# Gate and up projections of a decoder step: when the normed tokens are asked for, where the last splits stand, and in which order the quarter products run

## The chip, the cores and the metric

One core of a Trainium2 chip. The metric is the device time of one execution in microseconds (us). Engines: TensorE (PE) multiplies and writes accumulators in PSUM, VectorE (DVE), ScalarE (ACT) and GpSimd (POOL) work element by element, SyncE (SP) asks for transfers.

## The reference, cut to what matters

One layer of a decoder for 520 tokens (512 of a prompt, 8 samples), width 1024: mLSTM and retention heads, a cross-attention, and then the part that the change touches, a SwiGLU network of inner width 2816:

```python
hf = rmsnorm(x, g_ffn)
x = x + (jax.nn.silu(hf @ w_gate) * (hf @ w_up)) @ w_down
y = rmsnorm(x, g_final)
```

## The kernel before, in words

All tokens lie feature-major: 128 features on the partitions, 520 tokens along the free dimension, so x is 8 blocks of 128 x 520 (`X`). Each float32 operand of a product is split in a high part (ScalarE copies it to fp32r) and a low part (VectorE subtracts the high part from the raw one), and a product is hi·hi + hi·lo + lo·hi. `split` writes both; its lines are L191 (high) and L192 (low). The weights come in one long stream of blocks (`W`); `W.get` loads a block ahead into `wraw`, casts it (`whi`, L208) and subtracts (`wlo`, L209). A product that is not of the feed-forward's normed tokens but of `A` = x·g (also split) takes the row factors of the norm (`r_bc`, `r_h`) afterwards.

The inner width is 22 blocks of 128 columns. The first four (`PLAIN`) are plain projections: `proj(A, "pfg")` and `proj(A, "pfu")`, 48 matmuls each (8 row blocks, 3 products, 2 halves of 260 tokens), read out of PSUM by L1194 (gate, times the row factors), L1200 (up) and L1201 (their product, after Silu). An accumulator pair comes from `ps2`, of which there are two; the next projection but one needs the one that these lines empty.

Meanwhile the operands of the other 18 blocks are made: `operands` multiplies x by gain and row factors (L1152, eight operations into `xn`), forms sums of quarters (L1157, L1158, L1161, L1164) and splits seven of them into `xs` (`xsplit`). It is a generator: `spawn` puts it on the list of tasks, and each `step` runs it up to its next yield; `proj` makes a step after every second row block but the last.

Blocks 4 to 21 treat gate and up weights as a 2 x 2 matrix of quarters and make its product with the tokens by seven quarter products (j = 0 to 6) of 12 matmuls, with sums before (`weight_operands`: L1175 to L1178, seven splits, for the block after the running one) and after (L1221 to L1234). Products 2 and 3 go to the pair `ab`, 5 and 6 to `cd`, the others to single accumulators.

The results are split again (`ff_split`) as operands of the down projection. Those of the first 8 blocks go to `A` while later blocks run. Those of blocks 8 to 21 go to `TT`, the memory in which `xs` lies, and so can't be written before the last quarter block: `ff_split(KB + z)` writes over the operand of product z // 2. In the last block two of them are written after each product. The down projection follows (L1257; the last row block L1295), reading `A` for its first 8 row blocks and `TT` for the other 14.

The tile framework places the waits and sets the order of each engine's queue when the kernel is built (`schedule_with_timeline_sim=True`), from the order in which the operations are written and from when they are ready; each engine then runs its queue in that order.

Of the kernel before, what the change touches and what calls it, by code (L numbers as in the profile page):

```python
# [13 lines left out]
AF = mybir.ActivationFunctionType  # L14
ALU = mybir.AluOpType
# [10 lines left out]
KB = 8  # L26
# [3 lines left out]
H2 = N // 2  # L30
# [5 lines left out]
FB = DFF // P  # L36
# [79 lines left out]
def halves(ap):  # L116
    return ap.rearrange("p (a b) -> p a b", a=2)
# [23 lines left out]
def decoder_step(ctx: ExitStack, tc: tile.TileContext, i: dict, o: list):  # L141
    nc = tc.nc
    pe, act, dve, pool, sp = nc.tensor, nc.scalar, nc.vector, nc.gpsimd, nc.sync
# [18 lines left out]
    def ps2(name):  # L162
        return acc.tile([P, 2, 512], F32, tag="acc", name=name)

    def ps1(name):
        return psums[-1].tile([P, 512], F32, tag="msc", name=name)
# [21 lines left out]
    def split(hi, lo, src, scale=None):  # L188

        if scale is None:  # L190
            act.copy(hi, src)  # L191
            dve.tensor_tensor(lo, src, hi.bitcast(F32), ALU.subtract)  # L192
        else:
            act.activation(hi, src, AF.Copy, scale=scale)
            dve.scalar_tensor_tensor(lo, src, scale, hi.bitcast(F32), ALU.mult, ALU.subtract)

    def wraw(at, n):
        raw = wp.tile([P, KB * P], F32, tag="wraw", name="wraw", bufs=3)
        sp.dma_start(raw[:, :n], i["weights"][at : at + P * n].rearrange("(p n) -> p n", p=P))
        return raw  # L200
# [29 lines left out]
    def spawn(gen, group=None):  # L230
        tasks.append([gen, 0, group])
# [15 lines left out]
    def proj(x, name, order=range(KB), ahead=1):  # L247
        hi, lo = W.get(ahead)
        ps = ps2(name)
        for n, k in enumerate(order):  # L250
            mm_k(ps, hi, lo, x, k, k, n == 0, n == KB - 1)
            if n % 2 and n < KB - 1:
                step()
        return ps
# [109 lines left out]
    with ExitStack() as mx:  # L364
# [179 lines left out]
        def qkv_tiles(n):  # L544
            return [qkv.tile([P, N], F32, tag=t, name=f"{t}{n}") for t in ("q", "k", "v")]
# [222 lines left out]
        for h in range(4):  # L768
            q, k, v = qkv_tiles(f"m{h}")
# [16 lines left out]
        for h in range(4):  # L786
            q, k, v = qkv_tiles(f"r{h}")
# [7 lines left out]
        for hb in range(KB):  # L795
            ps = proj(A, "pgt")
# [60 lines left out]
    for ob in range(KB):  # L857

        ps = proj(B, "pwo", range(KB) if ob < KB - 1 else (*range(4, KB), *range(4)))
# [244 lines left out]
    for (k0, nk, nc_), need in zip(PASSES, (1, 2, 3)):  # L1104
        while min(done[0], attended[0]) < need or any(t[2] == "mem" for t in tasks):
            step()
        for c0 in range(0, D, nc_):
            hi, lo = W.get()
            for c in range(0, nc_, P):
                ob = (c0 + c) // P  # L1110
                ps = ps2("pwc")
# [23 lines left out]
    FR = fp.tile([P, FB - KB, N], F32, name="FR")  # L1135
# [7 lines left out]
    def ff(s, k, ts):  # L1143
        return A[:, s, k, ts] if k < KB else TT[:, k - KB, s, ts]

    def xsplit(j, x):
        split(*xs[j], x)

    def operands():

        for k in range(KB):
            dve.scalar_tensor_tensor(xn[:, :, k], halves(X[:, k]), vec[:, k, V_GF : V_GF + 1], r_h, ALU.mult, ALU.mult)  # L1152
            if k % 2:
                yield 1
        b11, b21, b12, b22 = (xn[:, a, k : k + 4].rearrange("p k n -> p (k n)") for a in range(2) for k in (0, 4))
        t3 = fr[:, 12 * N : 14 * N]
        dve.tensor_tensor(t3, b22, b12, ALU.subtract)  # L1157
        dve.tensor_tensor(b12, b12, b11, ALU.subtract)  # L1158
        xsplit(0, b11)
        yield 1  # L1160
        dve.tensor_tensor(b11, b22, b12, ALU.subtract)  # L1161
        xsplit(4, b21)
        yield 1
        dve.tensor_tensor(b21, b21, b11, ALU.subtract)  # L1164
        for j, x in ((1, t3), (6, b22), (3, b12), (2, b11), (5, b21)):
            xsplit(j, x)
            yield 1

    def weight_operands(out):

        g, u = (wraw(W.next()[1], KB * P) for _ in range(2))
        yield 1
        s13, s24 = (wp.tile([P, KB * P], F32R, tag=t, name="wsum", bufs=2).bitcast(F32) for t in ("whi", "wlo"))
        a11, a12, a21, a22, s3, s1, s2, s4 = (t[:, z : z + 4 * P] for t in (g, u, s13, s24) for z in (0, 4 * P))
        dve.tensor_tensor(s3, a11, a21, ALU.subtract)  # L1175
        dve.tensor_tensor(s1, a21, a22, ALU.add)
        dve.tensor_tensor(s2, s1, a11, ALU.subtract)
        dve.tensor_tensor(s4, a12, s2, ALU.subtract)  # L1178
        for w in (a11, s3, s2, s1, a12, a22, s4):
            hi, lo = (tp.tile([P, 4 * P], F32R, tag="q" + t, name="q" + t, bufs=8) for t in ("hi", "lo"))  # L1180
            split(hi, lo, w)
            out.append((hi, lo))
            yield 1

    def ff_split(f, raw):
        split(ff(0, f, slice(None)), ff(1, f, slice(None)), raw)

    spawn(operands())
    ops = []
    for f in range(PLAIN):  # L1190
        ps = proj(A, "pfg")
        gu = tp.tile([P, 4, H2], F32, tag="gu", name="gu").rearrange("p (a z) n -> p a (z n)", a=2)
        g, u = gu[:, 0], gu[:, 1]
        dve.tensor_tensor(halves(g), ps[:, :, :H2], r_h, ALU.mult)  # L1194
        act.activation(g, g, AF.Silu)
        if f == PLAIN - 1:
            spawn(weight_operands(ops))
        step()
        ps = proj(A, "pfu", ahead=int(f < PLAIN - 1))
        dve.tensor_tensor(halves(u), ps[:, :, :H2], r_h, ALU.mult)  # L1200
        dve.tensor_tensor(FR[:, f], u, g, ALU.mult)  # L1201
        step()
    drain()
    for f in range(PLAIN, FB):
        last, nxt = f == FB - 1, []
        more = weight_operands(nxt) if not last else iter(())
        next(more, None)
        ab, cd = ps2("pfa"), ps2("pfb")
        ps = [*(ps1(z)[:, :H2] for z in ("pfc", "pfd")), ab[:, 0, :H2], ab[:, 1, :H2], ps1("pfe")[:, :H2], cd[:, 0, :H2], cd[:, 1, :H2]]
        gu = tp.tile([P, 4, H2], F32, tag="gu", name="gu")  # L1210
        g1, g2, v1, v2 = (gu[:, z] for z in range(4))
        for j, (out, (wh, wl), (xh, xl)) in enumerate(zip(ps, ops, xs)):
            for k in range(4):
                for w, x in ((wh, xh), (wh, xl), (wl, xh)):
                    pe.matmul(  # L1215
                        out, w[:, k * P : (k + 1) * P], x[:, k * H2 : (k + 1) * H2],
                        start=k == 0 and w is wh and x is xh, stop=k == 3 and w is wl,
                    )
            next(more, None)
            if j == 0:  # L1220
                act.copy(g1, out)  # L1221
            elif j == 2:
                dve.tensor_tensor(g2, out, g1, ALU.add)
                dve.tensor_tensor(v1, ps[1], g2, ALU.add)
            elif j == 3:
                dve.tensor_tensor(gu[:, 1::2], out.unsqueeze(1).broadcast_to([P, 2, H2]), gu[:, 1:3], ALU.add)  # L1226
            elif j == 4:
                dve.tensor_tensor(g1, out, g1, ALU.add)
                act.activation(g1, g1, AF.Silu)
            elif j == 6:  # L1230
                dve.tensor_tensor(gu[:, 1:3], cd[:, ::-1, :H2], gu[:, 1:3], ALU.add)
                act.activation(g2, g2, AF.Silu)
                to = FR[:, f - KB if f >= KB else f]
                dve.tensor_tensor(halves(to), gu[:, 0:2], gu[:, 2:4], ALU.mult)  # L1234
            if f - PLAIN < KB and j == 5:
                ff_split(f - PLAIN, FR[:, f - PLAIN])
            if last:
                if j == 1:
                    W.fill(1)
                for z in (2 * j, 2 * j + 1):  # L1240
                    ff_split(KB + z, FR[:, z])
        list(more)
        ops = nxt
    tp_cm.__exit__(None, None, None)
# [4 lines left out]
    for obs in ((0, 1), *((ob,) for ob in range(2, KB - 1))):  # L1249
        pss = [ps2("pfd") for _ in obs]  # L1250
        for k0 in range(0, FB, KB):
            for ps in pss:
                hi, lo = W.get()
                for k in range(k0, min(k0 + KB, FB)):
                    for w, s in ((hi, 0), (hi, 1), (lo, 0)):
                        for a in range(2):
                            pe.matmul(  # L1257
                                ps[:, a, :H2], w[:, k - k0], ff(s, k, slice(a * H2, (a + 1) * H2)),
                                start=k == 0 and w is hi and s == 0, stop=k == FB - 1 and w is lo,
                            )  # L1260
        for ob, ps in zip(obs, pss):
            xb = X[:, ob]
            dve.tensor_tensor(halves(xb), halves(xb), ps[:, :, :H2], ALU.add)
            square(yp, ob)
            act.activation(xb, xb, AF.Copy, scale=vec[:, ob, V_GO : V_GO + 1])
# [20 lines left out]
    for n0, n in ((0, H2), (H2, N - H2)):  # L1286
        ts = slice(n0, n0 + n)
        ps = ps2("pfd")[:, 0, :n]
# [84 lines left out]
```

## Time and profile before

| | us |
|---|---|
| median of 3 runs | 884.39 (880.81 to 885.61) |
| the profiled execution | 878.44 |
| its span | 876.7 |
| PE, DVE, ACT busy in it | 835.8, 673.4, 397.5 |

The span goes from the first to the last instruction of the profiled execution; 1.7 us lie around it. A busy engine is one that has an instruction in it: the matmuls are pipelined, so a busy PE is not PE at its peak.

### The profile page before, as it was taken

What the parts mean: (1) busy time and instruction counts of PE and PEld (TensorE: products, weight loads), DVE (VectorE), ACT (ScalarE), POOL (GpSimd) and SP (SyncE); (2) the same over time, 40 slices, a digit from 0 to 9 for tenths busy, and PEclk for the clock granted to TensorE, in tenths of its full rate; (3) what the DMA queues carried; (4) which work ended last, traced back from release to release, by engine and by line L of the source; (5) the groups of instructions that cost most, each with busy time, mean ns of one, the idle gap of its engine ahead of it and who ended that gap; (6) DMA issues with size and microseconds to landing.
All of it is one profiled execution on the core that took longest, in us unless ns stands there. A gap on an engine that the chain in (4) does not pass through costs nothing.

```text
span 876.7 us, 16989 instructions
## 1 busy us (share of the span) xinstructions
PE 835.8 (95%) x6707; PEld 818.4 (93%) x6707; DVE 673.4 (77%) x1512; ACT 397.5 (45%) x791; POOL 179.6 (20%) x185
## 2 busy tenths in 40 slices
PE   6989989999999999999999879999999996999996
PEld 5989989999999999889999879999999996999995
DVE  6999998877786687876888897999999997232234
ACT  5545525434546353365442654555444555132231
POOL 5555332222024301415323400000000000011010
PEclk9999999999999999999999999999999998999998
DMA  8333323434345436784764222223333332222222
GB/s 272 99 97 124 104 76 122 124 99 124 103 146 193 121 124 215 250 301 118 233 208 140 73 66 79 97 97 100 119 119 99 96 105 84 84 91 91 84 67 98
DMA packets 32680, 110.56 MB, mean 126 GB/s; under 512 B 4000, under 2 KB 6176, under 8 KB 32344
## 3 DMA queue, kind: packets, MB, share of 16 engines
q1 hardware_dynamic: 27216, 95.80, 34.5%
q0 software_dynamic: 3616, 12.34, 3.9%
q10 hardware_dynamic: 1768, 1.34, 0.5%
q8 instruction: 53, 0.87, 0.4%
q14 instruction: 27, 0.22, 0.1%
HBM read 100.38 MB, written 9.07 MB: 125 GB/s over the span
## 4 chain that ended last, share of the span: by engine, by line
PE 76%; DVE 15%; DMA 4%; issue 2%; ACT 1%; POOL 1%; SPq 0%; DVEq 0%; ACTq 0%; POOLq 0%
PE pfd L1257 13%; PE pfa L1215 6%; PE pfb L1215 6%; PE pgt L223 5%; PE pcq L223 5%; PE pwo L223 5%; PE pwc L223 4%; PE pfc L1215 3%; PE pfe L1215 3%; PE prp L223 3%; PE ppl L223 3%; PE pfg L223 3%; PE pfd L1215 3%; PE pfu L223 2%; DVE cv L518 2%
## 5 line engine op out<-in xcount | busy, mean ns | idle before, releaser
L208 ACT CAST whi<-wraw 128x1024 fp32r<-128x1024 f32 (+1 forms) x104 | 107.2, 1032 | 179.6 <-PE pfd L1257 69.4
L209 DVE TENSOR_TENSOR wlo<-wraw,whi 128x1024 fp32r<-128x1024 f32 (+1 forms) x85 | 110.3, 1300 | 72.0 <-ACT whi L208 70.2
L302 POOL TENSOR_TENSOR ssq<-ssq,sq 128x520 f32<-128x520 f32 x18 | 28.8, 1600 | 369.1 <-ACT sq L301 363.9
L191 ACT CAST qhi<-wsum 128x512 fp32r<-128x512 f32 x72 | 42.9, 619 | 54.4 <-DVE wsum L1175 45.8
L1257 PE MATMUL pfd<-TT,whi 128*128 128x260 f32 x392 | 62.8, 282 | 0.0
L209 POOL TENSOR_TENSOR wlo<-wraw,whi 128x1024 fp32r<-128x1024 f32 x19 | 45.6, 2398 | 66.2 <-ACT whi L208 61.1
L1215 PE MATMUL pfa<-TT,qhi 128*128 128x260 f32 x288 | 53.7, 284 | 0.0
L1257 PEld LDWEIGHTS pfd<-TT,whi 128*128 128x128 f32 x392 | 53.7, 188 | 0.0
L1215 PE MATMUL pfb<-TT,qhi 128*128 128x260 f32 x288 | 53.0, 283 | 0.0
L192 DVE TENSOR_TENSOR qlo<-wsum,qhi 128x512 fp32r<-128x512 f32 x72 | 47.8, 684 | 0.0
L223 PE MATMUL pwc<-B,whi 128*128 128x260 f32 x256 | 43.7, 287 | 4.0 <-DVE X L291 3.0
L223 PE MATMUL ppl<-A,whi 128*128 128x260 f32 x256 | 45.4, 290 | 0.6 <-DVE up L510 0.6
L223 PE MATMUL pcv<-A,whi 128*128 128x260 f32 x256 | 45.0, 291 | 0.5 <-ACT whi L208 0.5
L1215 PEld LDWEIGHTS pfb<-TT,qhi 128*128 128x128 f32 x288 | 44.5, 188 | 0.0
L1215 PEld LDWEIGHTS pfa<-TT,qhi 128*128 128x128 f32 x288 | 44.4, 188 | 0.0
L223 PE MATMUL prp<-A,whi 128*128 128x260 f32 x256 | 44.2, 288 | 0.0
L223 PE MATMUL pgt<-A,whi 128*128 128x260 f32 x256 | 44.0, 287 | 0.0
L1257 PE MATMUL pfd<-A,whi 128*128 128x260 f32 x224 | 37.1, 289 | 6.0 <-DVE gu L1226 6.0
L223 PE MATMUL pcq<-A,whi 128*128 128x260 f32 x256 | 42.0, 283 | 0.0
L1215 PE MATMUL pfa<-TT,qlo 128*128 128x260 f32 x144 | 41.0, 285 | 0.7 <-DVE qlo L192 0.7
L223 PE MATMUL pwo<-B,whi 128*128 128x260 f32 x256 | 41.3, 283 | 0.0
L1215 PE MATMUL pfb<-TT,qlo 128*128 128x260 f32 x144 | 40.8, 283 | 0.0
(434 smaller groups left out, 2614.2 us busy)
## 6 DMA issues: line engine op xcount, KB each, us to landing
wraw<-in_weights_dram SPq DMA_DIRECT2D x132, 512.0 KB, 3.8
kv<-in_cache_k_dram SPq DMA_DIRECT2D x16, 512.0 KB, 4.5
kv<-in_cache_v_dram SPq DMA_DIRECT2D x16, 512.0 KB, 4.3
wraw<-in_weights_dram SPq DMA_DIRECT2D x8, 384.0 KB, 3.0
X<-in_x_dram SPq DMA_DIRECT2D x2, 1040.0 KB, 6.0
Cs<-in_state_C_dram POOLq DMA_DIRECT2D x4, 512.0 KB, 5.0
out_dram<-Cs POOLq DMA_DIRECT2D x4, 512.0 KB, 3.1
Ss<-in_state_S_dram POOLq DMA_DIRECT2D x4, 512.0 KB, 4.2
```

The costliest lines, as they stand in the source:

```text
L191: act.copy(hi, src)
L192: dve.tensor_tensor(lo, src, hi.bitcast(F32), ALU.subtract)
L208: act.copy(hi[:, :n], raw[:, :n])
L209: (pool if index in LO_ON_POOL else dve).tensor_tensor(lo[:, :n], raw[:, :n], hi[:, :n].bitcast(F32), ALU.subtract)
L223: pe.matmul(ps[:m, a, :H2], w[:, k, c0 : c0 + m], x[:, s, xk, a * H2 : (a + 1) * H2], start=first and w is hi and s == 0, stop=last and w ...
L302: (dve if ob == KB - 1 else pool).tensor_tensor(ssq, ssq, s, ALU.add)
L518: dve.scalar_tensor_tensor(cv[:, :LO], up[:, j : j + LO], wc(j), cv[:, :LO], ALU.mult, ALU.add)
L1215: pe.matmul(out, w[:, k * P : (k + 1) * P], x[:, k * H2 : (k + 1) * H2], start=k == 0 and w is wh and x is xh, stop=k == 3 and w is wl,)
L1257: pe.matmul(ps[:, a, :H2], w[:, k - k0], ff(s, k, slice(a * H2, (a + 1) * H2)), start=k == 0 and w is hi and s == 0, stop=k == FB - 1 and ...
```

## The change

Three things. The generator `operands` is spawned after the first gate block has been read (after L1194 and its Silu), not ahead of the plain blocks; its splits come in the order of the products. The order of the seven quarter products becomes a11, a12, s3, s2, s1, a22, s4 (it was a11, s3, s2, s1, a12, a22, s4), with the readings placed to match. In the last quarter block no results are split before product 4; after products 4, 5 and 6 two each are split (six of the 14), and the other eight within the down projection, one after every second row block; `W.fill(1)` moves from product 1 to product 3.

```diff
         xsplit(0, b11)
         yield 1
         dve.tensor_tensor(b11, b22, b12, ALU.subtract)
-        xsplit(4, b21)
+        xsplit(1, b21)
         yield 1
         dve.tensor_tensor(b21, b21, b11, ALU.subtract)
-        for j, x in ((1, t3), (6, b22), (3, b12), (2, b11), (5, b21)):
+        for j, x in ((2, t3), (3, b11), (4, b12), (5, b21), (6, b22)):
...
-        for w in (a11, s3, s2, s1, a12, a22, s4):
+        for w in (a11, a12, s3, s2, s1, a22, s4):
...
-    spawn(operands())
+    unsplit = list(range(KB, FB))
+
+    def rest_split(n):
+        for _ in range(min(n, len(unsplit))):
+            f = unsplit.pop(0)
+            ff_split(f, FR[:, f - KB])
+
     ops = []
     for f in range(PLAIN):
...
         act.activation(g, g, AF.Silu)
+        if f == 0:
+            spawn(operands())
         if f == PLAIN - 1:
             spawn(weight_operands(ops))
...
-        ps = [*(ps1(z)[:, :H2] for z in ("pfc", "pfd")), ab[:, 0, :H2], ab[:, 1, :H2], ps1("pfe")[:, :H2], cd[:, 0, :H2], cd[:, 1, :H2]]
+        pc, pd, pe_ = (ps1(z)[:, :H2] for z in ("pfc", "pfd", "pfe"))
+        ps = [pc, pd, ab[:, 0, :H2], ab[:, 1, :H2], pe_, cd[:, 0, :H2], cd[:, 1, :H2]]
...
             if j == 0:
-                act.copy(g1, out)
-            elif j == 2:
-                dve.tensor_tensor(g2, out, g1, ALU.add)
-                dve.tensor_tensor(v1, ps[1], g2, ALU.add)
+                act.copy(g2, out)
+            elif j == 1:
+                dve.tensor_tensor(g1, out, g2, ALU.add)
+                act.activation(g1, g1, AF.Silu)
             elif j == 3:
+                dve.tensor_tensor(g2, out, g2, ALU.add)
+                dve.tensor_tensor(v1, ps[2], g2, ALU.add)
+            elif j == 4:
                 dve.tensor_tensor(gu[:, 1::2], out.unsqueeze(1).broadcast_to([P, 2, H2]), gu[:, 1:3], ALU.add)
-            elif j == 4:
-                dve.tensor_tensor(g1, out, g1, ALU.add)
-                act.activation(g1, g1, AF.Silu)
...
             if last:
-                if j == 1:
+                if j == 3:
                     W.fill(1)
-                for z in (2 * j, 2 * j + 1):
-                    ff_split(KB + z, FR[:, z])
+                if j > 3:
+                    rest_split(2)
...
                                 start=k == 0 and w is hi and s == 0, stop=k == FB - 1 and w is lo,
                             )
+                    if k % 2:
+                        rest_split(1)
```

## Rows read from the trace of the kernel before

**Rows 1.** Chain of waits in order of time, 500 to 740: start, us, engine, operation.

```profile
511.16 7.54 PE pfg L223 x48
518.69 5.77 PE pfu L223 x48
...
547.53 1.45 PE pfc L1215 x12
...
630.28 1.44 PE pfd L1215 x12
...
711.08 1.45 PE pfd L1215 x12
...
737.78 2.29 PE pfd L1257 x9
```

**Rows 2.** Whom TensorE waited for: us in total, times, longest.

```profile
PE pfd L1257 <- DVE gu L1226: 6.0, 1, 6.0
PE pfg L223 <- DVE gu L1194: 4.4, 1, 4.4
PE pwc L223 <- DVE X L291: 3.0, 2, 2.7
...
PE pfa L1215 <- DVE qlo L192: 0.7, 1, 0.7
...
PE pfe L1215 <- ACT qhi L191: 0.6, 1, 0.6
```

**Rows 3.** TensorE by stretch: length, busy (count), granted clock, DMA share, GB/s.

```profile
495.00:506.00 11.00, 11.00 (x91) 1.00 0.29 77
...
512.00:515.00 3.00, 3.00 (x16) 0.50 0.00 0
...
738.00:740.00 2.00, 2.00 (x10) 0.50 0.00 0
```

**Rows 4.** VectorE in order of time at the first plain block: start, length.

```profile
506.29 4.11 DVE L1152 SCALAR_TENSOR_TENSOR FR<-X,vec,r_bc 128x520 f32<-128x520 f32 x6
510.32 0.69 DVE L1194 TENSOR_TENSOR gu<-pfg,r_bc 128x520 f32<-128x520 f32 x1
510.93 1.42 DVE L1152 SCALAR_TENSOR_TENSOR FR<-X,vec,r_bc 128x520 f32<-128x520 f32 x2
512.27 0.69 DVE L1200 TENSOR_TENSOR gu<-pfu,r_bc 128x520 f32<-128x520 f32 x1
512.88 1.22 DVE L209 TENSOR_TENSOR wlo<-wraw,whi 128x1024 fp32r<-128x1024 f32 x1
514.01 1.24 DVE L192 TENSOR_TENSOR TT<-FR,TT 128x1040 fp32r<-128x1040 f32 x1
515.16 1.24 DVE L1157 TENSOR_TENSOR FR<-FR 128x1040 f32<-128x1040 f32 x1
```

**Rows 5.** VectorE by stretch, plain blocks: length, busy (count), granted clock, DMA share.

```profile
506.00:534.00 28.00, 27.78 (x32) 0.94 0.21 65
```

**Rows 6.** All engines by stretch, quarter blocks and after: length; PE, PEld, DVE, ACT, POOL.

```profile
559.00:719.00 160.00, 160.00 (x1329) 159.85 (x1329) 152.60 (x270) 78.64 (x158) 0.00 (x0) 1.00 0.33 106
719.00:738.00 19.00, 11.72 (x92) 11.06 (x91) 18.97 (x32) 12.88 (x24) 0.00 (x0) 0.89 0.33 104
738.00:850.00 112.00, 112.00 (x925) 112.00 (x926) 30.59 (x31) 31.38 (x37) 8.70 (x5) 0.99 0.26 82
```

**Rows 7.** VectorE in order of time, last quarter block: first and last splits, readings.

```profile
722.64 1.30 DVE L192 TENSOR_TENSOR TT<-FR,TT 128x520 fp32r<-128x520 f32 x2
...
729.31 0.42 DVE L1223 TENSOR_TENSOR gu<-pfa,gu 128x260 f32<-128x260 f32 x1
...
734.44 0.42 DVE L1224 TENSOR_TENSOR gu<-pfd,gu 128x260 f32<-128x260 f32 x1
...
735.12 1.91 DVE L192 TENSOR_TENSOR TT<-FR,TT 128x520 fp32r<-128x520 f32 x3
736.94 0.69 DVE L1226 TENSOR_TENSOR gu<-pfa,gu 128x520 f32<-128x520 f32 x1
```

## The prediction

> **What bounds the kernel now.** I read the chain of waits in order of time first [rows 1]. From the plain blocks to the end of the down projection it is TensorE nearly throughout: a plain projection of 48 matmuls is 5.77 us, and in the quarter blocks the same product comes round every 10.10 us (630.28 to 711.08 is 8 blocks), with nothing between. So inside this stage a faster VectorE or ScalarE buys nothing; only the places where TensorE stands are worth anything. The second view lists whom TensorE waits for [rows 2]. Its two long waits of this stage are the two that the diff touches: 4.4 us for the reading L1194 of the first gate block and 6.0 us for the reading L1226 of the last quarter block; 0.7 and 0.6 us more stand just ahead of the latter. The third view is the granted clock of stretches [rows 3]: behind both waits TensorE runs at 0.50, the lower level (1.2 GHz), for some three us. Undisturbed it has 1.00 (2.4 GHz), and the 2.7 us wait ahead of the gate projections [rows 2] cost no such thing: the projections from 495 to 506 run at 1.00 [rows 3]. The last views are VectorE's operations in order of time around both waits, and its busy time by stretch [rows 4 to 7].
>
> **The front: normed tokens asked for later.** TensorE finished the first up block at 506.76 (511.16 less the 4.4 us wait), and needs the accumulator that L1194 empties. L1194 had its row factors at 506.29, but six operations L1152 stand ahead of it on VectorE, 4.11 us, so it runs at 510.32 [rows 4]. The change spawns the eight L1152 after L1194. Then L1194 takes 506.29 to 506.98, and 0.15 us later (as 511.01 to 511.16 now) the second gate block starts: 507.13 in place of 511.16, 4.0 us. The wait left is 0.4 us, well under the 2.7 us that left the clock up, so the 48 matmuls take 5.77 us and not 7.54 [rows 1]: another 1.8 us. That block ends at 512.90 and not 518.69, 5.8 us sooner.
>
> Nothing is removed from VectorE, though. It is busy 27.78 of the 28.00 us from 506 to 534 [rows 5], and TensorE now asks sooner. What is late next is the second up block, whose accumulator L1200 frees. Behind L1194 (0.61 us to the next start) stand eight L1152 at 0.685 each (4.11 over 6), so L1200 starts at 512.38, ends at 513.07, and the block starts at 513.2: a wait of 0.3 us. Its weights' low half is next: the high half is cast in time, since the subtraction runs at 512.88 now, right after L1200 [rows 4]; behind L1200 it runs from 512.99 to 514.2, while the block asks for it after four matmuls, at 513.7. That is 0.6 us more. If the first split of the tokens (L192, 1.15 us) gets in ahead of it, 1.75. Then VectorE still has ten or so operations of 1.15 us each, so the reading and the low half for the third gate block may come 0 to 1.6 us late in their turn. I take 0.3, 0.6 and 0.9, together 1.8: they lie between no wait (lower bound 0) and, as upper bound, a wait at each of the five blocks that follow of one 1.15 us operation, 5.8, which would eat everything. By 534 the list is as empty as now, since it holds the same work without a hole in both cases; the quarter blocks' sums (L1175) wait for the fourth gate block and move with TensorE. Front: 5.8 - 1.8 = 4.0 us, bounds 0 and 5.8.
>
> Which order VectorE's queue has decides this. In [rows 4] the low half at 512.88 belongs to the next projection, and yet it stands ahead of L1157, which was written one projection earlier: the scheduler that fills the queues takes what is ready, so a chain of dependent operations (L1157, L1158, L1161, L1164) lets later work in between. That is why I take waits of tenths and not of several operations.
>
> The Trainium skill (TensorE: Matmul & The Clock Gate, section Architectural detail) says that VectorE and ScalarE run their queues as strict FIFO. The trace agrees: L1194, which had all it needed at 506.29, ran behind the six that were queued first. By that rule with a queue filled as written the time would be the first rival's 878.8, with the order that the rows show it is the 873.8 of the sum.
>
> **The middle: plain gate quarters first.** The order of the seven products and of their seven weight operands changes, not their number: 84 matmuls, three 260-wide adds, three 520-wide operations, one copy and two Silu per block as before. The first two products then need only the raw quarters, not sums. Of the accumulators, the pair ab was emptied by operations after products 3 and 4, and now by two adds after product 4; the next block wants it at its product 3, some 7 us later. The pair cd is emptied at product 7 as now. TensorE already fills its 160.00 us of 160 there, VectorE 152.60 [rows 6], so a gain is excluded and a loss needs VectorE to lose its 7.4 us of room. I take 0; bounds 0 and +22 (third rival).
>
> **The end: last splits behind the readings.** Eighteen blocks of 10.10 us from 547.53 end at 729.3; the down projection starts at 737.78 [rows 1], so 8.5 us lie in the last block: 6.0 waiting for L1226, 1.3 for weight operands [rows 2], the rest in small change. VectorE is busy 18.97 us of the 19.00 [rows 6]. Ahead of L1226 it runs 13 of the 14 splits of the down projection's operand, from 722.64 to 735.12, at 0.61 us (1.30 for two, overlapped): 7.9 us. It also shows how a reading gets stuck: L1224 needs only L1223, yet comes 5.1 us behind it (729.31 to 734.44), with splits and others in between [rows 7]. The change writes no split before the operation that frees ab, six after products 5 to 7, and eight into the down projection, where VectorE is busy 30.59 us of 112 [rows 6]. With none ahead, ab would be free at 737.63 - 7.9 = 729.7 and TensorE would go straight on: 8 us. But the splits are ready early (the operand slots are free after each product), and [rows 4] showed that ready work written later still gets in. With 8 ahead the gain is 5 x 0.61 = 3.0. I take four or five ahead: 5.4 us. The remaining wait is then some 3 us or comes in pieces, so the clock stays up: the first 9 matmuls of the restart took 2.29 us [rows 1] at the 0.50 of [rows 3], where 9 x 0.120 (5.77 / 48) are 1.1, so 1.2 us come back. The first split needed in the down projection is of its ninth row block, after 16 row blocks of 0.72 us (5.77 / 8), 11.5 us on; the splits left are 8 x 0.61 = 4.9 us, hidden under that. The first down weights are asked for two products later; they have a whole projection's room. End: 5.4 + 1.2 = 6.6 us, bounds 3.0 and 9.7.
>
> **Sum.** 4.0 + 0 + 6.6 = 10.6 us. The profiled execution took 878.44 (span 876.7) and would take 867.8. The median of the three runs is 884.39, 6 us above it, and the runs spread by 4.8; I put the difference on the median: 873.8 us.
>
> **Rivals.**
> First, the front goes to VectorE: if its queue keeps the written order, the second up block's low half stands behind L1201, L1157, L1158 and a split (0.61 + 3 x 1.15), ends at 518.3 and TensorE waits 4.7 us there, enough to drop the clock as the 4.4 us did. Then the front gives 5.8 - 0.3 - 4.7 - 1.8 = -1.0, the end 6.6: 884.39 - 5.6, about 878.8. For it: the 27.78 of 28.00. Against: the mixed order of [rows 4].
> Second, the end is not what it says: the splits still fill VectorE ahead of the last readings, since they are ready, and nothing holds them back but place in the text. The end then gives about 0.5 of small change, the front 4.0: 879.9. For it: the 18.97 of 19.00 and L1224's delay; against: fewer are written in time.
> Third, on the other side: the new product order makes TensorE wait in each quarter block. The price is that of the last block now, 0.7 + 0.6 [rows 2], where VectorE has no room left: 1.3 us in 17 blocks is 22 us, and less the 10.6 of both ends that is 895.8. It decides from 0.88 us per block on ((10.6 + 4.4) / 17). Against it: VectorE's work per block is the same, with 0.46 us of room (7.4 / 16), and the sums get more time.
> Fourth, both ends come to nothing together: 884.
>
> **How the numbers follow.** A measurement here tells about 0.5% (4.4 us) from no change. Forecast as above: 0.62, range 869 to 879. First rival 0.12 and second 0.14, each a little more often beyond 4.4 us than not; third 0.07; fourth 0.05. Faster: 0.62 + 0.08 + 0.09 = 0.79; same: 0.04 + 0.05 + 0.05 = 0.14; slower 0.07. The range takes in the first two rivals and the largest gains: 867 to 883.
>
> **What would show it.** Right: L1194's successor runs before any L1152, TensorE's wait there falls under 1 us, no stretch at 0.50 follows; waits of some tenths appear for L1200 and low halves of weights in the plain blocks, and the quarter blocks start about 4 us sooner; they still come every 10.10 us; the wait of the first down matmul falls under 3 us, with splits inside the down projection. Wrong: a 4 us wait at the second up block (first rival); 13 splits still ahead of the last reading (second); a period above 10.5 us (third). A shift in stages ahead of 500 us, which the diff does not touch, would be outside all of these.

## The result, and the profile after

The changed kernel takes 877.99 us (median of 11 runs, 874.8 to 882.17), the kernel before 883.97 (11 runs beside it, 880.81 to 887.71): ratio 0.9947, 95% interval 0.9926 to 0.9968, so 0.5% faster, 4.7 us. The two medians lie 6.0 us apart, a little more than the ratio says and inside its interval; from here on the ratio on record is used, and microseconds beside a ratio are that share of some 882 us. Forecast were 873.8 us, 1.2%; the measured median lies inside the range of 867 to 883. The profiled execution took 874.8 us.

```profile
span 873.0 us, 17065 instructions
PE 833.0 (95%) x6707; PEld 816.0 (93%) x6707; DVE 671.6 (77%) x1512; ACT 406.7 (47%) x798; POOL 179.4 (21%) x185
```

That is the head of the page after. ScalarE is busy 9.2 us longer than the 397.5 of before, though no line of the diff gives it work: the first sign of what went wrong.

Lines have moved: L1194 of before is L1200 now, L1200 is L1208, the pair `ab` is read by L1235 and L1236 (it was last read by L1226), `cd` by L1240, the down projection is L1266. The waits of TensorE in the changed stages, after (us in total, times, longest):

```profile
PE pfb L1224 <- DVE gu L1240: 2.4, 1, 2.4
...
PE pfd L1266 <- DVE gu L1236: 1.1, 1, 1.1
...
PE pfg L223 <- DVE gu L1200: 0.4, 1, 0.4
...
PE pfu L223 <- DVE wlo L209: 0.3, 1, 0.3
```

Set beside [rows 2]: the 4.4 us at the first gate block have become 0.4, and the 6.0 us ahead of the down projection 2.4 and 1.1. VectorE at the first plain block, after (start, length), to be held against [rows 4]:

```profile
505.42 0.70 DVE L1200 TENSOR_TENSOR gu<-pfg,r_bc 128x520 f32<-128x520 f32 x1
506.04 5.45 DVE L1152 SCALAR_TENSOR_TENSOR FR<-X,vec,r_bc 128x520 f32<-128x520 f32 x8
511.40 0.69 DVE L1208 TENSOR_TENSOR gu<-pfu,r_bc 128x520 f32<-128x520 f32 x1
512.01 1.21 DVE L209 TENSOR_TENSOR wlo<-wraw,whi 128x1024 fp32r<-128x1024 f32 x1
```

The reading (L1200) goes ahead of all eight L1152, and the low half of the weights follows the second reading at once. Stretches of TensorE, after (length, busy and count, granted clock, DMA share, GB/s), against [rows 3]:

```profile
507.00:511.00 4.00, 4.00 (x35) 1.00 0.00 0
...
728.00:740.00 12.00, 12.00 (x102) 1.00 0.21 67
```

Both places that ran at 0.50 before now run at 1.00. And the quarter blocks, all engines (as [rows 6]):

```profile
559.00:719.00 160.00, 159.76 (x1331) 159.55 (x1330) 152.38 (x271) 82.66 (x165) 0.00 (x0) 1.00 0.35 105
```

So nearly every sign that the prediction asked for is there, and still, by the ratio, less than half of the gain arrived. One step did not hold even here: the working took four or five of the 14 last splits to run ahead of the last reading of `ab`, and VectorE after shows ten ahead of L1236 (13 stood ahead of L1226 in [rows 7]):

```profile
715.06 0.70 DVE L192 TENSOR_TENSOR TT<-FR,TT 128x520 fp32r<-128x520 f32 x1 [1.06 <-PE pfc L1224]
...
716.29 0.69 DVE L192 TENSOR_TENSOR TT<-FR,TT 128x520 fp32r<-128x520 f32 x1
...
719.65 2.52 DVE L192 TENSOR_TENSOR TT<-FR,TT 128x520 fp32r<-128x520 f32 x4
...
722.69 0.69 DVE L1240 TENSOR_TENSOR gu<-pfb,gu 128x520 f32<-128x520 f32 x1
723.30 0.42 DVE L1235 TENSOR_TENSOR gu<-pfa,gu 128x260 f32<-128x260 f32 x1
723.63 2.52 DVE L192 TENSOR_TENSOR TT<-FR,TT 128x520 fp32r<-128x520 f32 x4
...
727.21 0.42 DVE L1236 TENSOR_TENSOR gu<-pfa,gu 128x260 f32<-128x260 f32 x1
```

To see where the gain went, cut the span at the starts of three operations: T, the first of the two operations that finish the row factors (L278), ahead of everything that the diff touches; the first down matmul; and the second matmul pair of the last norm (`pn`). These are single profiled executions, and one comparison of stages is good to about a microsecond:

```
us              T to down   down to last norm   last norm to end
before            232.3          123.7               15.2
after             223.1          122.5               22.9
after - before     -9.2           -1.2               +7.7
```

Ahead of the last norm 10.4 us were won, where the sum had 10.6. Then 7.7 us are lost in a stage that the diff does not touch. ScalarE in order of time, after, in the last quarter block and in that tail:

```profile
718.87 1.28 ACT L1254 ACT_TABLE_LOAD   x1
...
724.38 1.28 ACT L1233 ACT_TABLE_LOAD   x1
...
731.32 0.42 ACT L1241 ACTIVATE gu<-gu 128x260 f32<-128x260 f32 x1 [2.37 <-DVE gu L1240]
...
850.65 1.28 ACT L273 ACT_TABLE_LOAD   x1 [2.47 <-PE pn L1288]
851.95 0.48 ACT L273 ACTIVATE nrml<-pn,vec 128x260 f32<-128x260 f32 x1
852.44 1.28 ACT L275 ACT_TABLE_LOAD   x1
853.74 0.42 ACT L275 ACTIVATE nrml<-nrml 128x260 f32<-128x260 f32 x1
```

and the same engine before:

```profile
739.59 0.63 ACT L191 CAST TT<-FR 128x520 fp32r<-128x520 f32 x1 [0.77 <-DVE FR L1234]
740.23 1.28 ACT L1245 ACT_TABLE_LOAD   x1
...
862.04 0.48 ACT L273 ACTIVATE nrml<-pn,vec 128x260 f32<-128x260 f32 x1 [2.48 <-PE pn L1277]
862.55 0.42 ACT L275 ACTIVATE nrml<-nrml 128x260 f32<-128x260 f32 x1
```

Read them like this. Before, the load of the table set for Ln and Exp (L1245) ran at 740.23, behind the last Silu and the last cast, and the norm's Ln (L273) and Exp (L275) found it in place. After, the same load (L1254) runs at 718.87, ahead of the last two Silu (L1233, L1241). L1233 has to bring the Silu table back at 724.38. From then on the set is gone, and at the end each Ln and each Exp loads a table of its own, on the chain that ends last. Why an Exp does not find its table in what the Ln just ahead of it has loaded, no run here shows. ScalarE grouped by line, after (busy us and mean ns, idle ahead):

```profile
L273 ACT ACT_TABLE_LOAD x3 | 3.8, 1283 | 2.5 <-PE pn L1288 2.5
L275 ACT ACT_TABLE_LOAD x3 | 3.8, 1283 | 0.1
```

Six loads of 1.283 us are 7.7 us, the whole loss of the tail; with the Silu table's they are 9.0 of ScalarE's 9.2 us. The Trainium skill (ScalarE: Activation LUTs, section What ACT_TABLE_LOAD costs) gives 1283 ns for the load and, with a drain, 2.66 us in all for every switch of sets. The load agrees (1283 ns in the rows above); the drain does not show here: the Ln starts 1.30 us after its load starts (850.65 to 851.95), and the load of the Exp starts 0.01 us after the Ln ends (852.43 to 852.44). As an estimate from the page's 2.66 us, six switches would have made the tail 16 us longer, and it grew by 7.7.

Why it moved: the line behind the last quarter block, `tc.keep_in_program_order(act.preload_act_table_set(LOG_EXP))`, holds the load behind the ScalarE instruction written just ahead of it. Before, that was the cast of block 21's result, which needs the last Silu, and the load follows it at once (739.59, 740.23). After, it is the cast of the sixth of the 14 results, block 13's, which is ready as soon as the third product of the last block has read its operands.

### The profile page after: what moved, and what is told of

Read it like the earlier page. It is cut to its first block, busy times and chain, and to the rows that moved or that the text cites. A ratio compares the mean times of both kernels' runs of the same rounds, so it can differ in the third digit from the quotient of the medians.

```text
span 873.0 us, 17065 instructions
## 1 busy us (share of the span) xinstructions
PE 833.0 (95%) x6707; PEld 816.0 (93%) x6707; DVE 671.6 (77%) x1512; ACT 406.7 (47%) x798; POOL 179.4 (21%) x185
## 4 chain that ended last, share of the span: by engine, by line
PE 73%; DVE 16%; DMA 4%; ACT 3%; issue 2%; POOL 1%; SPq 0%; DVEq 0%; ACTq 0%; POOLq 0%
PE pfd L1266 13%; PE pfb L1224 6%; PE pfa L1224 6%; PE pcq L223 5%; PE pgt L223 4%; PE pwc L223 4%; PE ppl L223 4%; PE pwo L223 3%; PE pfc L1224 3%; PE pfd L1224 3%; PE prp L223 3%; PE pfe L1224 3%; PE pfu L223 2%; DVE cv L518 2%; DVE wlo L209 2%
## 5 line engine op out<-in xcount | busy, mean ns | idle before, releaser
L1266 PE MATMUL pfd<-TT,whi 128*128 128x260 f32 x392 | 62.8, 283 | 0.0
L1224 PE MATMUL pfb<-TT,qhi 128*128 128x260 f32 x288 | 52.8, 283 | 2.4 <-DVE gu L1240 2.4
L1266 PEld LDWEIGHTS pfd<-TT,whi 128*128 128x128 f32 x392 | 53.7, 188 | 0.0
L1224 PE MATMUL pfa<-TT,qhi 128*128 128x260 f32 x288 | 53.1, 282 | 0.0
L1224 PEld LDWEIGHTS pfb<-TT,qhi 128*128 128x128 f32 x288 | 44.4, 188 | 2.6 <-ACT TT L191 2.6
L1224 PEld LDWEIGHTS pfa<-TT,qhi 128*128 128x128 f32 x288 | 44.3, 188 | 0.0
L1224 PE MATMUL pfb<-TT,qlo 128*128 128x260 f32 x144 | 40.7, 283 | 0.0
L223 PEld LDWEIGHTS pwc<-B,whi 128*128 128x128 f32 x256 | 35.8, 188 | 5.3 <-DVE X L291 3.7
L1224 PE MATMUL pfa<-TT,qlo 128*128 128x260 f32 x144 | 40.5, 281 | 0.0
```

What stands on the lines that cost most here:

```text
L223: pe.matmul(ps[:m, a, :H2], w[:, k, c0 : c0 + m], x[:, s, xk, a * H2 : (a + 1) * H2], start=first and w is hi and s == 0, stop=last and w ...
L1224: pe.matmul(out, w[:, k * P : (k + 1) * P], x[:, k * H2 : (k + 1) * H2], start=k == 0 and w is wh and x is xh, stop=k == 3 and w is wl,)
L1266: pe.matmul(ps[:, a, :H2], w[:, k - k0], ff(s, k, slice(a * H2, (a + 1) * H2)), start=k == 0 and w is hi and s == 0, stop=k == FB - 1 and ...
```

## The experiments

The theory after this: the front is as forecast, the end's gain is real, and the third part costs 7.7 us through the displaced load. Rivals: that the tail has another reason, and that the end's gain comes from the product order and not from the splits. All kernels compute the whole reference. Products are counted from one here and below, as in the prediction: product 4 is j = 3 in the code. Summary first (ratios to the kernel before, run beside each, with 95% intervals; the difference of the medians departs from the ratio by up to 1.3 us; stages in us as above, from one profiled execution each):

```
kernel                                     ratio  interval          T-down  down-norm  tail
after                                      0.9947 0.9926 - 0.9968   223.1    122.5     22.9
e1 after, load behind last Silu            0.986  0.9831 - 0.9889   224.0    122.2     15.2
e5 before, load ahead of last Silu         1.0099 1.0067 - 1.013    232.8    125.1     23.0
e3b splits later alone, load as changed    1.0078 1.0053 - 1.0104   232.9    124.0     23.0
e3 splits later alone, load behind Silu    0.9992 0.9972 - 1.0013   232.3    125.1     15.4
e2 front alone                             0.995  0.9928 - 0.9972   228.8    125.2     15.3
e4 product order alone                     0.993  0.9909 - 0.9951   229.4    122.2     15.2
e7 front and order, no third part          0.9878 0.9829 - 0.9927   224.0    122.2     15.1
e8 e1, splits queued behind a reading      0.9838 0.9783 - 0.9892   219.4    123.8     15.1
e10 e3, splits queued behind a reading     0.9897 0.9869 - 0.9926   225.5    123.3     15.3
```

**The load behind the last Silu (e1).** The changed kernel with one line moved.

```diff
                 act.activation(g2, g2, AF.Silu)
+                if last:
+                    tc.keep_in_program_order(act.preload_act_table_set(LOG_EXP))
...
     tp_cm.__exit__(None, None, None)
-    tc.keep_in_program_order(act.preload_act_table_set(LOG_EXP))
```

> The changed kernel with one line moved: the activation-table load written after the down projection's start is now written behind the last Silu of the last quarter block. Theory A (the change's missing microseconds are table loads: the load ran ahead of the last two Silu, so these called their own table back, and each Ln and Exp of the last norm then loads a table, six times 1.28 us on the last chain): no load in the last norm, the stretch from the last norm matmul's start to the end is 15.2 us as before the change and not 22.9, and the time is some 7 to 8 us under the changed kernel's, a ratio near 0.987 to the kernel before. Theory B (the tail is longer because the output transfers or the last products were shifted by the splits inside the down projection): the tail stays near 22.9 us and the ratio stays near 0.995.

870.63 us, ratio 0.986. ScalarE in order of time:

```profile
735.75 0.42 ACT L1241 ACTIVATE gu<-gu 128x260 f32<-128x260 f32 x1 [2.36 <-DVE gu L1240]
736.19 1.28 ACT L1243 ACT_TABLE_LOAD   x1
...
855.75 0.48 ACT L273 ACTIVATE nrml<-pn,vec 128x260 f32<-128x260 f32 x1 [2.48 <-PE pn L1289]
```

The load stands behind the last Silu again, no Ln or Exp loads a table, and the tail is back at 15.2 us. The edit moves only this load; the gain over the changed kernel, 0.87% (0.9947 less 0.986) of 884, is 7.7 us. The two intervals together leave that figure some 3 us of play either way; the stage, 22.9 against 15.2 us, is the sharper measure.

**The load alone, in the kernel before (e5).** The opposite test: nothing of the change, only the load written before the last block's last Silu.

```diff
+            if last and j == 5:
+                tc.keep_in_program_order(act.preload_act_table_set(LOG_EXP))
...
     tp_cm.__exit__(None, None, None)
-    tc.keep_in_program_order(act.preload_act_table_set(LOG_EXP))
```

> The kernel before with one line moved: the table load of the last norm is written ahead of the last Silu of the last quarter block instead of behind the block. Nothing of the change is in it. Theory A (table loads are the price): one Silu calls its table back, the last norm makes six loads of 1.28 us, all on the last chain, so 7.7 us more, ratio 1.0087. Theory B (the loads are covered by the wait for products and sums): ratio 1.000 to 1.003.

889.8 us, 1.0099: 1% slower by one moved load. Its table loads in the list by line:

```profile
L273 ACT ACT_TABLE_LOAD x3 | 3.8, 1283 | 2.5 <-PE pn L1278 2.5
L275 ACT ACT_TABLE_LOAD x3 | 3.8, 1283 | 0.1
...
L1236 ACT ACT_TABLE_LOAD x1 | 1.3, 1283 | 0.0
...
L1229 ACT ACT_TABLE_LOAD x1 | 1.3, 1283 | 0.0
```

The written load (L1236), the Silu table brought back (L1229), and the six of the norm: the pattern of the changed kernel, with its tail of 23.0 us. With e1 this settles the cause of the loss from both sides.

**The splits written later, alone (e3b and e3).** The kernel before with the third part of the change, once with the load left where it was written (e3b), once with the load of e1 (e3). The part that both share, without the definition of `rest_split`:

```diff
...
             if last:
-                if j == 1:
+                if j == 3:
                     W.fill(1)
-                for z in (2 * j, 2 * j + 1):
-                    ff_split(KB + z, FR[:, z])
+                if j > 3:
+                    rest_split(2)
...
+                    if k % 2:
+                        rest_split(1)
```

> The kernel before with the last part alone, as the change has it: six splits behind products 5 to 7, eight in the down projection, the table load left where it is written. With the load behind the last Silu the same part gave 0.9992. Theory A: the load is held only behind the ScalarE operation written just before it, which is now a split that is ready early and no longer the one that needs the last Silu; so six loads in the last norm and 7.7 us, ratio near 1.008. Theory B (the cost of the changed kernel comes only from parts together): ratio near 1.000.

> The kernel before with the last part alone (six splits behind products 5 to 7 of the last block, eight in the down projection), and the table load written behind the last Silu so that no load moves. The prediction's sum gives 6.6 us (5.4 of the wait for L1226 and 1.2 of clock), ratio 0.9925; by the second rival (splits still run ahead) 0.5 us, ratio 0.9995. The wait of the first down matmul, 6.0 us before, should be 1 to 3 us.

e3b: 888.38 us, 1.0078, so by itself the third part is a loss. e3: 881.61 us, 0.9992, so without the load it is nothing. VectorE of e3 in the last quarter block:

```profile
729.33 0.43 DVE L1230 TENSOR_TENSOR gu<-pfa,gu 128x260 f32<-128x260 f32 x1
...
734.47 0.42 DVE L1231 TENSOR_TENSOR gu<-pfd,gu 128x260 f32<-128x260 f32 x1
...
735.14 1.91 DVE L192 TENSOR_TENSOR TT<-FR,TT 128x520 fp32r<-128x520 f32 x3
736.97 0.70 DVE L1233 TENSOR_TENSOR gu<-pfa,gu 128x520 f32<-128x520 f32 x1
```

Against [rows 7] that is the same queue to within some hundredths of a microsecond: 13 splits still run ahead of the last reading of `ab`, and TensorE still waits 6.0 us for it. The splits were written later, but they are ready early, and they were put in the queue by that.

**The front alone (e2).** The kernel before with `spawn(operands())` behind the first Silu.

```diff
-    spawn(operands())
...
         act.activation(g, g, AF.Silu)
+        if f == 0:
+            spawn(operands())
```

> The kernel before with the first part alone: the normed tokens are spawned behind the first gate block's reading; order of products and splits as before. The prediction's sum gives 4.0 us for it (5.8 less 1.8 of new waits), ratio 0.9955; if VectorE's list eats it (the first rival), 0 to 1 us slower than the end of the plain blocks now, ratio 1.000. The stretch from the first L1152 operation to the first quarter matmul, 41.2 us before, should fall to about 37; the wait of 4.4 us for the first gate reading should be under 1 us, with no stretch at clock 0.50 behind it.

878.3 us, 0.995: 4.4 us (interval 2.5 to 6.4), where the sum had 4.0. The wait for the first reading is 0.4 us and no stretch at 0.50 follows. In the profiled execution the second quarter block comes only 3.6 us sooner, counted from T, than before (4.7 in the changed kernel), because at the third gate block TensorE waits 1.0 us for the low half of its weights:

```profile
PE pfg L223 <- DVE wlo L209: 1.0, 1, 1.0
```

The wait of 6.0 us at the down projection stands as before.

**The product order alone (e4).** The changed kernel with the spawn and the last block's splits as they were before: the reversed diffs of e2 and e3b.

> The kernel before with the middle part alone: a11, a12, s3, s2, s1, a22, s4 as order of the products, readings placed to match; the normed tokens asked for and the last splits written as before. The prediction's sum gives 0, ratio 1.000, and a period of 10.1 us per quarter block; the third rival would give a longer period (over 10.5 us). In the last block ab is then read by two adds after product 4 with the splits of the first three products written ahead, so its end may wait a microsecond more or less than the 6.0 us.

876.63 us, 0.993: 6.2 us from the part that was forecast at nothing. TensorE's 6.0 us wait for the reading is gone; in its place stands one of 3.0 us, earlier, for the pair `cd` (`pfb`), which the reading of the block before frees. VectorE of e4 around it:

```profile
732.24 0.69 DVE L1232 TENSOR_TENSOR gu<-pfb,gu 128x520 f32<-128x520 f32 x1
732.85 0.42 DVE L1227 TENSOR_TENSOR gu<-pfa,gu 128x260 f32<-128x260 f32 x1
...
736.15 0.42 DVE L1228 TENSOR_TENSOR gu<-pfa,gu 128x260 f32<-128x260 f32 x1
```

A reason can be read from the rows. Before, `ab` became free at the end of a chain of three dependent operations, L1223, L1224, L1226 [rows 7], and in each gap the queue let splits in: 729.31 to 736.94. Now two adds straight behind product 4 empty it, with one gap; ten splits stand ahead of L1228 where 13 stood ahead of L1226, and L1228 ends at 736.57, ahead of the down projection's start at 737.73. No run changes the length of this chain alone, so this stays a reading of the trace.

**Front and order, without the third part (e7).** The changed kernel with the reversed diff of e3b alone.

> The changed kernel without its last part: tokens asked for behind the first reading, new product order, the splits of the last block written as before, two after each product. If the parts add, front 0.995 and order 0.993 give 0.988, and no load stands in the last norm. If the last part was worth something beside its loads, it stays above the 0.986 of all three with the load mended; if the prediction's step were right (the moved splits bring the end's gain), 0.993 or more.

870.61 us, 0.9878. The gains of e2 and e4 add up (0.50% and 0.70% against 1.22%), and the stages are those of e1 within 0.1 us. Ten splits run ahead of the last reading of `ab` in both. So with the new order too, the splits written later bring nothing that these runs can tell.

**The splits held back in the queue (e8, e10).** If being ready is what brings the splits ahead, tying them must work where writing them later did not. e8 is e1, and e10 is e3, with VectorE's half of every one of the 14 splits tied behind a reading of `ab` (`issue_after` keeps what the block writes behind the named operation in that engine's queue): in e8 the second add behind product 4, in e10 the operation behind product 4 in the old order.

```diff
-                dve.tensor_tensor(v1, ps[2], g2, ALU.add)
+                read = dve.tensor_tensor(v1, ps[2], g2, ALU.add)
...
-                    rest_split(2)
+                    with tc.issue_after(read.ins):
+                        rest_split(2)
...
-                        rest_split(1)
+                        with tc.issue_after(read.ins):
+                            rest_split(1)
```

> All three parts, the table load behind the last Silu, and VectorE's halves of the 14 last splits tied in the queue behind the add that frees ab in the last block, so that they can't run ahead of it. In the kernel with the load alone mended TensorE still waits 3.0 us in the last block for a reading of the block before, with splits ahead of it on VectorE. If those splits are the cause, that wait goes, the stretch from the end of the row factors to the first down matmul falls by some 3 us from 224.0 to 221, ratio near 0.983. If the weight operands of the last block are the cause, the wait stays near 3 us and the ratio near 0.986; if the splits then come too late for the ninth row block, a new wait stands in the down projection some 11 us after its start.

> The last part alone with the old product order, as in the run that gave 0.9992, but now VectorE's halves of the 14 last splits are tied in the queue behind the operation that frees ab in the last block; the table load is behind the last Silu. If the splits ahead of that reading are what makes TensorE wait (the prediction's mechanism) and only writing them later was no means to move them, the 6.0 us wait goes, the stretch from the end of the row factors to the first down matmul falls from 232.3 to about 224 to 226, and the down projection keeps the upper clock: ratio 0.990 to 0.992. If the old product order itself is the cause (its chain of three dependent readings), the wait stays over 3 us and the ratio over 0.994. Behind the reading ten splits then stand ahead of the one that frees cd, so a wait of some 2 us may come up at the second down block.

e10: 873.23 us, 0.9897, against e3's 0.9992. VectorE of e10:

```profile
733.00 0.70 DVE L1233 TENSOR_TENSOR gu<-pfa,gu 128x520 f32<-128x520 f32 x1
733.62 6.19 DVE L192 TENSOR_TENSOR TT<-FR,TT 128x520 fp32r<-128x520 f32 x10
```

No split stands ahead of the reading any more, the 6.0 us wait is gone, and from T to the down projection are 225.5 us, 6.8 less than in e3. e8: 866.48 us, 0.9838, the fastest kernel of the study, and faster than the changed one. Whether it beats e1 the intervals leave open; in the profiled executions the way from T to the end is 3.0 us shorter (358.3 against 361.3). VectorE of e8:

```profile
729.95 0.42 DVE L1236 TENSOR_TENSOR gu<-pfa,gu 128x260 f32<-128x260 f32 x1
730.29 6.18 DVE L192 TENSOR_TENSOR TT<-FR,TT 128x520 fp32r<-128x520 f32 x10
...
738.83 0.69 DVE L1240 TENSOR_TENSOR gu<-pfb,gu 128x520 f32<-128x520 f32 x1
```

and what TensorE waits for at the down projection:

```profile
PE pfd L1268 <- ACT whi L208: 0.9, 1, 0.9
...
PE pfd L1268 <- DVE gu L1240: 0.2, 1, 0.2
```

The 3.0 us wait for `cd` is gone. Ten splits in one piece now hold up the reading of `cd`, and the second down block asks for it 0.2 us too early; the 0.9 us for a weight's high half is new as well.

## Why the prediction was right or wrong, by its steps

Three steps failed. The one that took away the gain is in the end's term, which counted the moved splits as VectorE work "hidden under" the down projection and so put their price at nothing: they displaced a table load, and that cost 7.7 us. The other two, "I take 0" for the middle and "I take four or five ahead" for the end, were wrong in opposite directions and nearly cancelled. That the gain ahead of the last norm came out at 10.4 us where the sum had 10.6, and that the measured median lies inside the range, is luck.

**Front: right.** The reading L1200 runs 505.42 to 506.12, 0.15 us later the second gate block starts, 1.64 us after T where it was 5.67: 4.0 us. The wait left is the 0.4 us of the working, and no stretch at 0.50 follows. The new waits were put at 1.8 us in three pieces. From the second to the third gate block pass 12.42 us (506.27 to 518.69) for two products of 5.77: 0.9 us, and the next product takes 5.80 (to 524.49). So the third piece, 0.9 us at later blocks, did not come in the changed kernel (in e2, with the old order of splits, it did: 1.0 us). The third gate block starts 4.9 us sooner, counted from T. The first rival, VectorE eating the front, fell with that: it needed the queue to be filled as written.

**Middle: the period right, the worth wrong.** TensorE fills 159.76 of 160 us, VectorE 152.38, so the third rival (a wait per block) is out. But "I take 0" failed. It looked at the new order only in the blocks where TensorE never waits. In the last block, the very place that the end's term is about, the order decides by how long a chain of dependent operations `ab` becomes free (three before, two now), and [rows 7] showed that each gap in the chain lets splits in. Alone the order is worth 0.7% (e4 measures that; that the shorter chain is why is a reading of its rows).

**End: the amount right, the cause wrong.** T to down projection and the clock behind it gave 9.2 and 1.2 us, front included, where 4.0, 5.4 and 1.2 were forecast. But "I take four or five ahead" failed as a statement about writing splits later: e3 has 13 ahead, as before, and with the new order there are ten, written later (changed kernel, e1) or not (e7). The second rival's mechanism was right, ready work fills the queue; its time was not, because the product order made good what the splits did not. What the step had put a price on, a reading with few splits ahead, is what e10 then measures: compared with before, 6.8 us to the down projection and 0.4 behind it, where 5.4 and 1.2 were put. That a remaining wait of some 3 us leaves the clock up did not hold either: the waits of 3.0 us in e1, e4 and e7 each brought 0.50.

**What was put at nothing: the load.** The end's term counted the VectorE half of the moved splits (8 x 0.61) and hid it under the down projection. The ScalarE half of a split was never looked at, nor the instruction of L1245 that was held behind the last of them. Missed was 7.7 us, six loads of 1.28, shown by e1, e5 and e3b. With the load put right, e1 is 1.4% faster than before, interval 1.1 to 1.7, and the forecast of 1.2% lies in it, by the luck named above.

**Loose ends.** In the profiled executions the stretch from T to the down projection loses 3.5 us in e2, 2.9 in e4 and 8.3 in e7, which is 1.9 more than the sum, though the ratios add up. The traces account for nearly all of it ahead of the quarter blocks: they come 3.6 us sooner than before in e2 but 4.7 in e7, because of the 1.0 us wait named above, and 0.6 us later in e4, where the second gate block takes 8.16 us and not 7.54 because the lower clock lasted longer behind the same 4.4 us wait. That TensorE waits 2.4 us for `cd` in the changed kernel and 3.0 in e1 is one split: six stand ahead of L1240 in the rows above, seven in e1. Open is whether e8 beats e1, and what a run with only the chain of readings shortened would give.

## What to carry to other kernels

When an instruction is pinned to "the one written just before it", check for every edit near it which instruction that now is; a table load that ran ahead of the last user of the old table was paid again here at six later uses, on the path that sets the end. Where a scheduler fills the queues by what is ready, writing work later did not move it: an ordering edge did (e10, e8), and so, as the rows of e4 read, did a shorter chain of readings before the accumulator is free. And read the tail of the trace even if the diff ends far ahead of it: here a net of 0.5% was a gain of over 1% and a loss of 0.9%.

## What the runs showed of the hardware that was not expected

One and the same wait ended differently. Ahead of the gate projections, in code that no kernel here changes, TensorE waits 2.7 us in every profiled execution. In five of them (before, after, e2, e3, e5) the granted clock then stays at 1.00 (2.4 GHz); in the six others (e1, e3b, e4, e7, e8, e10) it falls to 0.50 (1.2 GHz) for some 3.4 us. So the reading in the prediction that this wait "cost no such thing" held for that one execution only. The first matmuls behind the wait, before and in e8, and a stretch of e8 ([rows 3] has that of before):

```profile
492.67 0.74 PE L223 MATMUL pwc<-B,whi 128*128 128x260 f32 x4 [2.70 <-DVE X L291]
498.23 1.23 PE L223 MATMUL pwc<-B,whi 128*128 128x260 f32 x4 [2.69 <-DVE X L291]
500.00:501.00 1.00, 1.00 (x7) 0.50 0.00 0
```

This also parts the executions by T, which the experiments do not touch: it came at 504.3 to 505.5 us in the five and at 506.3 to 512.6 in the six, which is more than 3.4 us at half the clock, 1.7 us, explain. Differences between whole spans of single executions are worth little here, and the stages above are counted from T for that reason.

In the last quarter block the 2.4 us wait for `cd` in the changed kernel left the clock up, and the 3.0 us in e1, e4 and e7 brought the lower level. The first full stretch of TensorE behind the wait, after and in e1:

```profile
724.00:725.00 1.00, 1.00 (x11) 1.00 0.00 0
729.00:730.00 1.00, 1.00 (x6) 0.50 0.00 0
```

After what the same wait did at 2.7 us, these few cases give no length at which the clock falls.

Behind the same wait of 6.0 us the down projection lost unequal amounts: down to last norm takes 122.2 us undisturbed (e1, e4, e7), 123.7 before, but 125.1 in e3 and 125.2 in e2, so 1.5 to 3.0 us, where the sum had 1.2. The difference is how long the lower clock lasted once the matmuls had started again: 2.9 us before, 6.0 in e2 and in e3.
